# Dealing channels to partitions as 16 x 8 in a DMA-bound batch norm on Trainium2

## The chip, the cores and the metric

The kernel runs on one core of one Trainium2 chip. The metric is the device time of one execution in microseconds (us); lower is better. The kernel before takes 2485.87 us, the median of four runs.

## The reference

A batch norm with given statistics over `x` of shape 32 x 256 x 128 x 128 in float32, 512 MiB in and 512 MiB out:

```python
def reference(x, gamma, beta, running_mean, running_var):
    eps = 1e-5
    ...   # the four parameters reshaped to (1, 256, 1, 1)
    return gamma * (x - mean) / np.sqrt(var + eps) + beta
```

Each channel needs one scale and one shift. All the rest is moving data.

## The kernel before

One tile is half an image: 128 channels, one for each SBUF partition, 16384 elements (64 KiB) a row. There are 64 tiles, three buffers, and one queue (SyncE's) for all loads and stores. Groups of three tiles are loaded, computed in place with one `tensor_scalar` each, and stored.

```python
NBUF = 3
GROUPS = [3] * 20 + [2, 2]
...
    xr = x.rearrange("n (cb p) h w -> (n cb) p (h w)", p=P)
    outr = out.rearrange("n (cb p) h w -> (n cb) p (h w)", p=P)
...
    def load(i):
        t = data.tile([P, HW], f32, tag="t")
        nc.sync.dma_start(out=t[:], in_=xr[i])
        tiles[i] = t
...   # parameters: four rows of 256 loaded, turned in 32x32 blocks, scale and shift computed
    turned = params.tile([B, C], f32, tag="turned")
    nc.vector.transpose(out=turned[:], in_=rows[:])
...
    def store(i):
        t = tiles.pop(i)
        nc.sync.dma_start(out=outr[i], in_=t[:])

    first = 0
    for g, size in enumerate(GROUPS):
        idxs = range(first, first + size)
        for i in idxs:
            compute(i)
        for i in idxs:
            store(i)
        first += size
        ...   # the loads of the next group
```

## Time and profile before

| | before |
|---|---|
| time, median of 4 | 2485.87 us (2485.76 to 2486.37) |
| span of the profiled execution | 2483.6 us |
| VectorE busy | 566.0 us, 23% |
| rate of the DMA engines over the span | 432 GB/s |
| one 64 KiB row on one DMA engine | 2.418 us |

The last line comes from the packet records of the trace, which hold start, duration and size of each packet, but not its engine or addresses. The page and the views behind this, and how the row's time makes up the span, are shown in the prediction. In the same records 16 rows of 64 KiB are in flight for 2417 of the 2484 us, as many as the page counts engines.

### The profile page before, as it was taken

The page shows a single profiled execution, that of the slowest core. Times are in us where ns is not written, and L with a number is a line of the kernel's source. Part 1 is how long each engine was busy: PE and PEld are TensorE (multiplying, and loading weights), DVE is VectorE, ACT ScalarE, POOL GpSimd, SP SyncE. Part 2 cuts the span into 40 slices and gives each one's busy share as a digit, 9 for nine tenths or more (in the row PEclk, how much of TensorE's full clock was granted, in tenths as well). Part 3 has the DMA queues.
Part 4 walks back from the last instruction along what each step waited for, and adds up shares of the span by engine and source line. Part 5 has one row for each costly group of instructions (what it writes and reads, how often), then busy time and mean ns, then how long its engine had stood idle before and what let it go on. Part 6 is the DMA issues. An engine that isn't in the chain of part 4 may idle for free.

```text
span 2483.6 us, 383 instructions
## 1 busy us (share of the span) xinstructions
DVE 566.0 (23%) x75; ACT 1.6 (0%) x2; POOL 0.2 (0%) x4
## 2 busy tenths in 40 slices
DVE  3140404121221213140403121221213040403112
ACT  0000000000000000000000000000000000000000
POOL 0000000000000000000000000000000000000000
DMA  9999999999999999999999999999999999999999
GB/s 421 423 439 439 425 436 439 431 431 439 431 431 439 435 426 436 436 431 435 435 435 427 439 434 427 439 434 427 439 437 432 432 437 433 431 437 433 431 437 396
DMA packets 18442, 1073.77 MB, mean 432 GB/s; under 512 B 2052, under 2 KB 2056, under 8 KB 2056
## 3 DMA queue, kind: packets, MB, share of 16 engines
q1 hardware_dynamic: 18432, 1073.75, 99.9%
q14 instruction: 2, 0.02, 0.0%
q10 hardware_dynamic: 8, 0.00, 0.0%
HBM read 536.88 MB, written 536.87 MB: 432 GB/s over the span
## 4 chain that ended last, share of the span: by engine, by line
another core or an unknown queue 72%; DVE 22%; DMA 4%; issue 0%; DVEq 0%; SPq 0%
DVE t L93 22%; DMA t<-in_x_dram 4%; DVEq L93 0%; SPq L51 0%; SPq L104 0%
## 5 line engine op out<-in xcount | busy, mean ns | idle before, releaser
L93 DVE TENSOR_SCALAR t<-t,scale_t,shift_t 128x16384 f32<-128x16384 f32 x64 | 564.0, 8812 | 1863.9 <-DMA t<-in_x_dram 1863.8
L66 DVE STREAM_TRANSPOSE turned<-rows 32x256 f32<-32x256 f32 x1 | 0.4, 432 | 21.5 <-DMA rows<-in_running_mean_dram 21.5
L78 ACT ACT_TABLE_LOAD x1 | 1.3, 1283 | 2.6 <-issue 2.6
L71 DVE COPY par<-turned 32x8 f32<-32x8 f32 x4 | 0.6, 161 | 0.1
L56 DVE MEMSET rows<- 32x256 f32 x1 | 0.3, 272 | 0.8 <-PEq L132 0.8
L78 ACT ACTIVATE tmp_t<-par,eps_t 128x2 f32<-128x2 f32 x1 | 0.3, 297 | 20.0 <-DVE par L71 20.0
L85 DVE RECIPROCAL tmp_t<-tmp_t 128x2 f32<-128x2 f32 x1 | 0.2, 165 | 0.4 <-ACT tmp_t L78 0.4
L87 DVE TENSOR_TENSOR tmp_t<-par,scale_t 128x2 f32<-128x2 f32 x1 | 0.2, 161 | 0.0
L88 DVE TENSOR_TENSOR shift_t<-par,tmp_t 128x2 f32<-128x2 f32 x1 | 0.2, 161 | 0.0
L86 DVE TENSOR_TENSOR scale_t<-par,tmp_t 128x2 f32<-128x2 f32 x1 | 0.2, 160 | 0.0
L132 POOL MEMSET const-uint8-127<- 128x1 uint8 x1 | 0.1, 103 | 0.0
L132 POOL MEMSET const-bfloat16-1.0<- 128x1 bf16 x1 | 0.1, 101 | 0.0
L132 POOL MEMSET const-float32-0.0<- 128x1 f32 x1 | 0.1, 98 | 0.2 <-issue 0.2
L132 POOL MEMSET const-float32-1.0<- 128x1 f32 x1 | 0.1, 98 | 0.0
L64 DVE MEMSET eps_t<- 128x1 f32 x1 | 0.1, 59 | 0.0
## 6 DMA issues: line engine op xcount, KB each, us to landing
t<-in_x_dram SPq DMA_DIRECT2D x64, 58.0
out_dram<-t SPq DMA_DIRECT2D x64, 49.1
rows<-in_running_var_dram ACTq DMA_DIRECT2D x1, 1.0 KB
rows<-in_gamma_dram ACTq DMA_DIRECT2D x1, 1.0 KB
rows<-in_beta_dram ACTq DMA_DIRECT2D x1, 1.0 KB
rows<-in_running_mean_dram ACTq DMA_DIRECT2D x1, 1.0 KB
```

The costliest lines, as they stand in the source:

```text
L56: nc.vector.memset(rows, 0.0)
L64: nc.vector.memset(eps_t, eps)
L66: nc.vector.transpose(out=turned[:], in_=rows[:])
L71: nc.vector.tensor_copy(out=par[q * B : (q + 1) * B], in_=blocks[:, :, q, 0:4])
L78: nc.scalar.activation(out=tmp_t[:], in_=var_t, func=mybir.ActivationFunctionType.Sqrt, bias=eps_t[:], scale=1.0,)
L85: nc.vector.reciprocal(out=tmp_t[:], in_=tmp_t[:])
L86: nc.vector.tensor_mul(out=scale_t[:], in0=gamma_t, in1=tmp_t[:])
L87: nc.vector.tensor_mul(out=tmp_t[:], in0=mean_t, in1=scale_t[:])
L88: nc.vector.tensor_sub(out=shift_t[:], in0=beta_t, in1=tmp_t[:])
L93: nc.vector.tensor_scalar(out=t[:], in0=t[:], scalar1=scale_t[:, cb : cb + 1], scalar2=shift_t[:, cb : cb + 1], op0=mybir.AluOpType.mult, ...
L132: nc = _bacc.Bacc("TRN2", target_bir_lowering=False, num_devices=1)
```

## The change

The intent is that the 16 DMA engines work side by side on 1 MiB of the tensor. Partition `e * 8 + k` now holds channel `k * 16 + e` of its half, so an engine that takes the eight partitions of one `e` reads channel `e`, then `16 + e`, and so on, while its neighbours read the channels beside it. That each engine takes one `e` is an assumption behind the change; no record names the engine of a packet. The parameters have to be put in the same order, which costs one small VectorE copy.

```diff
-    xr = x.rearrange("n (cb p) h w -> (n cb) p (h w)", p=P)
-    outr = out.rearrange("n (cb p) h w -> (n cb) p (h w)", p=P)
+    NE = 16
+    NK = P // NE
+    xr = x.rearrange("n (cb k e) h w -> (n cb) e k (h w)", k=NK, e=NE)
+    outr = out.rearrange("n (cb k e) h w -> (n cb) e k (h w)", k=NK, e=NE)
...
+    lined = params.tile([B, C], f32, tag="lined")
+    nc.vector.tensor_copy(
+        out=lined.rearrange("p (cb e k) -> p cb e k", e=NE, k=NK),
+        in_=rows.rearrange("p (cb k e) -> p cb e k", k=NK, e=NE),
+    )
     turned = params.tile([B, C], f32, tag="turned")
-    nc.vector.transpose(out=turned[:], in_=rows[:])
+    nc.vector.transpose(out=turned[:], in_=lined[:])
```

## The prediction

> **What bounds the kernel now.** I read the page first (engines, slices, queue), then the group table, then the SyncE queue's own waits, then the windows, and last the single packet records of the trace. The page's top says who is busy:
>
> ```profile
> span 2483.6 us, 383 instructions
> DVE 566.0 (23%) x75; ACT 1.6 (0%) x2; POOL 0.2 (0%) x4
> DMA  9999999999999999999999999999999999999999
> GB/s 421 423 439 439 425 436 439 431 431 439 431 431 439 435 426 436 436 431 435 435 435 427 439 434 427 439 434 427 439 437 432 432 437 433 431 437 433 431 437 396
> q1 hardware_dynamic: 18432, 1073.75, 99.9%
> HBM read 536.88 MB, written 536.87 MB: 432 GB/s over the span
> ```
>
> VectorE works 23% of the span. The DMA engines are at 9 tenths or more in each of the 40 slices, and the one queue that carries the tensor occupies the 16 engines for 99.9% of the span. The rate varies only from 421 to 439 GB/s between the first slice and the last but one. 18432 packets over 128 transfers (64 loads, 64 stores) are 144 each: 128 rows of 64 KiB and 16 small closing packets[...]. So each engine carries 8 rows of a transfer.
>
> ```profile
> L93 DVE TENSOR_SCALAR t<-t,scale_t,shift_t 128x16384 f32<-128x16384 f32 x64 | 564.0, 8812 | 1863.9 <-DMA t<-in_x_dram 1863.8
> t<-in_x_dram SPq DMA_DIRECT2D x64, 58.0
> out_dram<-t SPq DMA_DIRECT2D x64, 49.1
> ```
>
> The compute instruction takes 8.8 us for a tile and waits 1864 us for loads, which costs nothing, since the DMA engines have no gap meanwhile. The waits of the SyncE queue show the same from the other side:
>
> ```profile
> SPq L104 <- DVE t L93: 1451.7, 64, 47.2
> SPq L51 <- DMA out_dram<-t: 950.3, 60, 19.3
> ```
>
> SyncE waits for data, yet three tiles' worth of transfers is always queued ahead of the engines. The windows view, over one group of three tiles in the middle and over the tail, gives the steady rate and the end:
>
> ```profile
> 1000.00:1116.00 116.00, 26.13 (x4) 0.00 (x0) 0.00 (x0) 1.00 1.00 434
> 2453.00:2483.60 30.60, 0.00 (x0) 0.00 (x0) 0.00 (x0) 1.00 0.83 358
> ```
>
> (Columns: length, busy time of VectorE, ScalarE and GpSimd, clock, DMA share, GB/s.) The packet records put a number on one row: of 16384 records of 65536 bytes, 14433 took 2418 ns to the nanosecond and only some 180 took 2450 or more. That is 65536 / 2418 = 27.1 GB/s for an engine, 433.7 for 16. Each engine moves 64 x 2 x 8 = 1024 rows, 1024 x 2.418 = 2476 us. The remaining 7.6 us of the span are start, tail and some slow packets, mostly where a group turns from loads to stores. So the kernel is bound by the pace of one row on one engine, everywhere.
>
> [...]
>
> **The change part by part.**
>
> *Parameters.* One VectorE copy of 32x256 is added. The memset of that shape took 272 ns and the transpose 432 ns, so I estimate 0.3 to 0.45 us with its strided read. It sits before the first tile's compute (25.0 us in the timeline). Then the queue still has two loads to carry, until about 62 us, while the first store is asked for at 33.8 us. Beside work, 0 us on the end.
>
> *Bytes, rows, instructions.* Unchanged: 64 loads and 64 stores, 128 rows of 64 KiB each. The built program writes a load as 128x1x16384 in SBUF from 16x8x16384 in DRAM, where it was 128x16384 on both sides.[...] The issue of a transfer (0.34 us) may grow; with the queue filled ahead it is hidden.
>
> *Addresses in DRAM.* [...] This is the intended gain. But a row already takes 27.1 GB/s, [...] all non-row time is 7.6 us. Gain from it at most 8 us, 0.3%.
>
> *Partitions per engine.* This is where I see the cost. [...] a row takes 2 x 2.418 = 4.836 us. Stores read the same partitions and suffer alike. 1024 x 4.836 = 4952 us, plus 7.6 = 4960 us at worst.
>
> [...] In before, the 16 engines' starts lie within 1 us of each other at first (0.4 of a row) and spread to about 2.4 us (one row) by the end. I take s = 0.4 to 0.7 as a mean: factor 2 - s/4 = 1.9 to 1.83, 2476 x 1.83 to 1.9 = 4530 to 4700, and 4950 with s near 0. The choice is 4750 us.
>
> **The rivals.**
>
> *A: nothing moves.* [...] the engines could fall into opposite phase (s = 4) early and stay there. Then only DRAM addresses differ: 2478 to 2490 us. For it: the intent only makes sense if somebody expected full rate; opposite phase would be kept once reached. Against: nothing in the queue (full at all times) creates such a lead, and the spread in before is a row, not four.
>
> *B: DRAM order hurts.* [...] It would give perhaps 2500 to 2800 us. Unlikely.
>
> *C: partial overlap.* A lead that wanders over all values, mean s = 2, gives factor 1.5: 3720 us. Possible[...].
>
> *D: the intended gain*: 2475 to 2480 us, within 2% in any case; over 2% faster would need 443 GB/s[...].
>
> **Range and chances.** [...] nearly in step (4300 to 4960) 0.62, wandering (3000 to 4300) 0.15, small loss from B 0.04; together slower 0.81. A and D together 0.18; faster by 2%, 0.01. The range 3000 to 4980 leaves out the unmoved kernel, which carries most of the remaining two in ten.
>
> **What would show it right or wrong.** Right: 64 KiB packets at about 4.8 us[...], instead of 2.418; GB/s in the slices 220 to 240; DMA still 9 tenths everywhere; the median landing of loads and stores about doubled (58 to some 110 us, 49 to some 95 us); the wait of L93's instruction for loads at some 4100 us; its 8.8 us unchanged; VectorE's share at 12%. Wandering leads would show as slices that rise in steps from 220 towards 430. B would show packets of mixed length, with reads and writes unequal. The prediction is wrong if packets remain at 2418 ns[...].

The sum: 1024 rows for an engine, each of 2 x 2.418 = 4.836 us, are 4952 us, and with the 7.6 us outside the rows 4960 us at worst. A lead of `s` rows of one engine on another lowers the factor of 2 by `s / 4`, so `s` of 0.4 to 0.7 gives 2476 x 1.83 to 1.9 = 4530 to 4700 us; opposite phase is a lead of four rows, half of the eight that an engine carries of a transfer. The choice was 4750 us. The factor of 2 and `s / 4` are assumptions, and only the row of 2.418 us, the 16384 rows over 16 engines and the 7.6 us come from the trace. The gain of at most 8 us likewise assumes that a row does not get shorter than 2.418 us. The 2500 to 2800 us of rival B are a guess.

## The result

The changed kernel takes 4587.2 us, the median of four runs (4549.3 to 4651.2). The ratio is 1.840, with a 95% interval of 1.828 to 1.852. A ratio is the mean time of one kernel's fast runs over that of the other's of the same rounds, so it is not quite the ratio of the medians quoted here. The profiled execution is the slowest of the four (4651 us). It is labelled slow because it lies more than 1.5% above the fastest; this kernel scatters by that much by itself, and the readings below are about a factor of nearly two.

The page of the changed kernel, the lines that answer to the first ones of before:

```profile
span 4649.2 us, 384 instructions
DVE 566.4 (12%) x76; ACT 1.6 (0%) x2; POOL 0.2 (0%) x4
DMA  9999999999999999999999999999999999999998
GB/s 208 235 211 257 235 252 226 228 240 223 239 219 246 226 240 219 241 224 240 227 232 230 226 239 224 245 227 251 223 241 223 240 235 233 233 229 244 201 223 204
q1 hardware_dynamic: 18432, 1073.75, 98.8%
HBM read 536.88 MB, written 536.87 MB: 231 GB/s over the span
```

The engines are as busy as before and the packets and bytes are the same, yet the rate is 231 GB/s in place of 432. So no wait was added; each packet takes longer. "Busy" in this view only says that a packet was in flight: the queue is at 98.8% at this rate.

The groups and the issues (after the bar: busy us, mean ns, then idle time before it; for an issue, the median us to landing):

```profile
L102 DVE TENSOR_SCALAR t<-t,scale_t,shift_t 128x16384 f32<-128x16384 f32 x64 | 564.0, 8812 | 3984.6 <-DMA t<-in_x_dram 3984.6
L70 DVE COPY lined<-rows 32x256 f32<-32x256 f32 x1 | 0.4, 364 | 38.3 <-DMA rows<-in_running_mean_dram 38.3
t<-in_x_dram SPq DMA_DIRECT2D x64, 113.5
out_dram<-t SPq DMA_DIRECT2D x64, 93.9
```

The compute instruction is unchanged at 8812 ns and waits 3985 us for loads, where it waited 1864. Landing went from 58.0 to 113.5 us for a load and from 49.1 to 93.9 for a store. Both directions suffer. The SyncE queue's own waits grew in the same proportion:

```profile
SPq L113 <- DVE t L102: 2724.0, 64, 83.6
SPq L55 <- DMA out_dram<-t: 1785.1, 60, 38.0
```

The parameters are not the cause. The timeline at the first tile:

```profile
39.41 0.36 DVE L70 COPY lined<-rows 32x256 f32<-32x256 f32 x1 [38.29 <-DMA rows<-in_running_mean_dram]
...
41.92 0.16 DVE L97 TENSOR_TENSOR shift_t<-par,tmp_t 128x2 f32<-128x2 f32 x1
44.30 8.81 DVE L102 TENSOR_SCALAR t<-t,scale_t,shift_t 128x16384 f32<-128x16384 f32 x1 [2.22 <-DMA t<-in_x_dram]
```

The added copy took 0.36 us and the shift was ready at 42 us. The first tile's data came only at 44.3 us, so the compute waited for data, not for parameters.

The packet records show the new term. In the first three loads (384 rows) the median row took 5.11 us and the shortest 4.21. Over the whole run the median is 4.99 us: 11834 of 16384 rows took 4.5 us or more, 1880 under 2.5 us, the rest between. Each transfer leaves 16 small closing packets, and as many semaphore events, in the trace; the first compute starts 0.1 us after the last of the 16 events of its load (44.2 and 44.3 us). Since there are 16 for each transfer and 16 rows in flight, I take them as one for each engine; the records name none. From the last of one transfer to the last of the next, the mean time is 39.1 us for a load and 33.5 for a store, where before it was 19.4 and 19.3. (The expectations below use 38.1 and 34.2. Those come from the closing packets in order of time, sixteen at a time, which mixes neighbouring transfers.) By this reading the engines do not stay together either. The closing packets of one load lie within 1.0 us in the first three loads and about 40 us apart by the seventh. Over all 128 transfers the median is 59 us, more than the 41 us that eight rows of 5.11 us take. Before, it was never over 4.2 us.

### The profile page after: what moved, and what is told of

The parts are those of the page before. It is cut to its first block, busy times and chain, and to the rows that moved or that the text cites. A ratio compares the mean times of both kernels' runs of the same rounds, so it can differ in the third digit from the quotient of the medians.

```text
span 4649.2 us, 384 instructions
## 1 busy us (share of the span) xinstructions
DVE 566.4 (12%) x76; ACT 1.6 (0%) x2; POOL 0.2 (0%) x4
## 3 DMA queue, kind: packets, MB, share of 16 engines
q1 hardware_dynamic: 18432, 1073.75, 98.8%
## 4 chain that ended last, share of the span: by engine, by line
another core or an unknown queue 86%; DVE 12%; DMA 1%; issue 0%; DVEq 0%
DVE t L102 12%; DMA t<-in_x_dram 1%; DVEq L102 0%
## 5 line engine op out<-in xcount | busy, mean ns | idle before, releaser
L102 DVE TENSOR_SCALAR t<-t,scale_t,shift_t 128x16384 f32<-128x16384 f32 x64 | 564.0, 8812 | 3984.6 <-DMA t<-in_x_dram 3984.6
## 6 DMA issues: line engine op xcount, KB each, us to landing
t<-in_x_dram SPq DMA_DIRECT2D x64, 113.5
out_dram<-t SPq DMA_DIRECT2D x64, 93.9
```

Of the source, the lines that this page charges most:

```text
L102: nc.vector.tensor_scalar(out=t[:], in0=t[:], scalar1=scale_t[:, cb : cb + 1], scalar2=shift_t[:, cb : cb + 1], op0=mybir.AluOpType.mult, ...
```

## The experiments

My theory was that the partitions are the cause: that some sets of partitions, when the engines reach them at the same time, slow the rows down. The main rival was the DRAM order: that rows which stand 64 KiB apart, side by side, are slower. A third suspect is the issue, which the change lengthened: the median record of a load on the SyncE queue went from 339 to 577 ns. No trace names the partition or the engine of a packet, so the theories can only be told apart by kernels.

The mechanism that I had in mind for the theory, and the name that went with it, are cut from the expectations below, since no run shows them. A forecast that follows a cut without a name is that of this theory. A pair is two engines that, by the theory, slow each other down; a lead is the head start of one on the other, in rows.

**The same deal, another DRAM order.**

```diff
-    xr = x.rearrange("n (cb k e) h w -> (n cb) e k (h w)", k=NK, e=NE)
+    xr = x.rearrange("n (e cb k) h w -> n cb e k (h w)", cb=NCB, e=NE)
```

(The output and the parameters follow.) The 16 steps of the pattern now stand 1 MiB apart in DRAM, each of eight neighbouring channels.

> The deal of the change (16 x 8 rows[...]) with another DRAM order[...]. [...] as slow as the change, 4450 to 4750 us, packets again in two heaps at 2.42 and about 5.05 us. DRAM-order theory (side-by-side 64 KiB steps hurt): near 2486 us, at most 2600.

It took 4544.9 us (2 runs), ratio 1.827; the results are correct. The slices of its page:

```profile
GB/s 211 230 212 265 229 269 232 236 246 228 243 221 252 227 253 227 243 228 239 235 235 240 230 243 225 257 220 253 225 259 231 234 234 238 241 228 246 209 226 207
```

The side-by-side order is gone and the loss stays. The packets are as in the changed kernel (11513 rows of 4.5 us or more, 2088 under 2.5), not in two clean heaps.

**Nearly the changed DRAM order, the plain 128 partitions.**

```diff
-    xr = x.rearrange("n (cb p) h w -> (n cb) p (h w)", p=P)
+    xr = x.rearrange("n (hf b c) (q h2) w -> (n hf) (c q) b (h2 w)", hf=2, b=4, q=4)
```

A partition holds a quarter channel of four channels; the scale table has eight columns and the compute is cut in four.

> The DRAM order of the change, nearly, with the plain 128-partition deal: a partition holds a quarter (16 KiB) of a channel[...], rows of 16 KiB. [...] 2475 to 2500 us, rows of 16 KiB at about 0.605 us. DRAM-order theory: slow, 3500 us or more.

It took 2506.5 us (4 runs), ratio 1.0078 (1.0062 to 1.0095), correct. That is just above my 2475 to 2500.

```profile
GB/s 410 431 430 431 430 431 429 431 431 431 430 430 431 430 432 429 431 430 431 430 431 430 431 430 431 431 430 431 430 431 430 431 430 432 430 431 429 431 430 379
```

Blocks of four partitions that stand 64 KiB apart in DRAM run at nearly the full rate, 429 GB/s over the span against 432. The 0.8% fits the shorter rows: four of 16 KiB take 4 x 0.611 = 2.444 us against 2.418 for one of 64 KiB. The order is only nearly that of the change, but the two runs together rule the side-by-side order out as the cause of the loss, and the halves below find the same loss in the DRAM order of before. A gain from it is not visible either.

**Engines set apart in time.** If the loss comes from what the engines reach at the same time, a head start for some of them should change it. I chose four rows, half of the eight that an engine carries of a transfer. Two small copies from DRAM to DRAM, queued first, are meant to delay 12 engines by four rows and then 4 of these by four more (the trace has 12 and then 4 closing packets for them, which I read as so many engines; it does not say which):

```diff
+    LEAD = 4
+    scratch = nc.dram_tensor("scratch", (16, LEAD + 1, HW), f32).ap()
+    images = x.rearrange("n c h w -> n c (h w)")
+    nc.sync.dma_start(out=scratch[4:16, 0:LEAD], in_=images[4:16, 0:LEAD])
+    nc.sync.dma_start(out=scratch[0:4, 0:LEAD], in_=images[0:4, 0:LEAD])
```

> The changed kernel with two small DRAM-to-DRAM copies queued ahead of everything, one on 12 engines and one on 4 of them[...]. [...] opposite phase, so 2500 to 2900 us, most packets at 2.42 us. DRAM-order theory[...]: 4400 to 4750 us as before.

It took 2631.0 us (2 runs), ratio 1.058, correct. The transfers, addresses and partitions are those of the changed kernel, and 1956 us of the loss are gone. The slices:

```profile
GB/s 346 423 419 437 430 430 430 430 431 430 432 429 433 429 430 426 426 434 426 434 426 434 429 428 433 427 433 430 431 429 436 432 429 433 430 430 314 238 225 201
```

The full rate holds for 36 slices and then falls to the changed kernel's. The closing packets of a transfer say why. Up to the last load before the stores of the first group of two tiles, the first of the last four closing packets comes 18.4 to 19.6 us after the first of all. Then these groups dissolve within one transfer. In the timeline there:

```profile
2398.07 8.81 DVE L108 TENSOR_SCALAR t<-t,scale_t,shift_t 128x16384 f32<-128x16384 f32 x1 [68.87 <-DMA t<-in_x_dram]
2406.91 19.94 SPq L119 DMA_DIRECT2D out_dram<-t  x2
```

The first store of the group is issued at 2406.9 us, when eleven of the 16 closing packets of the second and last load of the group are already out. I read this so: these eleven engines have nothing left to do and start this store together, and so the head start is lost. The transfers are slow from there on (314, 238, 225 and 201 GB/s in the last slices). They do not stay in step: the next two loads close over 45 us.

**The same with groups of three to the end.** `GROUPS = [3] * 21 + [1]`.

> The lead of 4 rows again, with groups of three tiles to the end and one tile last, in place of two groups of two. In the run with lead 4 the completions of a transfer kept the same spread until the first group of two, 2404 us, and lost it there: the leading engines run dry, because one queued tile (19.4 us) does not cover the spread (19.6 us) plus a compute (8.8 us), and then all start together. If that is the reason: 2500 to 2550 us. If the lead dies out of itself by that time: 2600 us or more.

It took 2561.7 us (4 runs, 2551 to 2582), ratio 1.031 (1.026 to 1.037), correct. That is just above my band of 2500 to 2550.

```profile
GB/s 335 413 420 432 432 434 432 436 431 433 432 436 432 433 433 427 433 429 433 432 430 432 432 431 429 434 428 432 428 435 431 426 435 429 430 432 436 426 416 146
```

The spread now stays until the last tile, whose lone store has nothing queued beside it and falls into the slice of 146 GB/s. So the reason given for the loss at the groups of two fits, and opposite phase does not die out by itself in 2.4 ms (426 to 436 GB/s from the fourth slice to the 38th). It does not beat the kernel before.

**A head start of two rows, and of eight.** The same diff with `LEAD = 2` and `LEAD = 8`.

> The same with a lead of 2 rows. [...] eight rows at a lead of s rows take 2 x (s x 2.42 + (4 - s) x 5.05) us, so 128 transfers at s = 2 take about 3825 us; with some drift 3300 to 4200 us. Theory without kept leads: 4400 to 4750 us.

> A lead of 8 rows, one whole turn of a transfer[...]. [...] 4400 to 4750 us, as without a lead. If any long lead frees the engines (for example by the distance in DRAM): 2500 to 2900 us.

Two rows: 4515.9 us (2 runs), correct. My rule, an estimate from fast rows of 2.42 us and slow ones of 5.05, by which the gain grows evenly with the head start, is wrong. It is not that the lead vanished at once: the closing packets of the second and third loads still come in groups 5 to 6 us apart. Yet between 50 and 100 us no row took less than 4.31 us, against 2.418 in before. This head start does not free these loads at all. (Its 5 to 6 us are two rows at the fast pace but only about one at 5 us a row; no other lead under four rows was tried.) The run is also the control for the copies themselves: with copies queued ahead, the time is still within 2% of the changed kernel's.

Eight rows: two runs, 2718.0 and 4332.0 us, correct. The midpoint means nothing; one execution went each way.

> The same kernel as the run with lead 8, whose two executions took 2718 and 4332 us, for its spread. If a pair can fall into opposite phase by chance and then stays: again a mix of executions near 2700 and near 4300 to 4600 us. If a long lead frees the engines as such: all near 2700. If one of the two executions was a disturbance: all like the other.

The four runs took 4427.7, 4416.5, 2720.0 and 4305.1 us. The granted clock is 1.0 in all, and both kinds came again: this kernel has two ways to go. Of six executions four stay near the changed kernel (two of them, 4305 and 4332 us, just below my band of 4400 to 4750) and two are near 2720 us. One of each kind was profiled, first the one of 2718 us, then the one of 4427.7:

```profile
GB/s 257 279 392 357 413 414 423 427 419 432 417 432 417 430 423 418 430 418 434 421 422 429 418 433 417 438 418 426 429 418 433 418 431 419 429 423 396 287 234 167
GB/s 239 364 315 335 286 252 258 253 223 243 220 254 218 254 221 254 223 252 223 247 224 246 225 243 232 242 232 234 236 233 237 232 239 229 246 225 248 209 226 211
```

In the first, the second transfer closes in three groups, at 0, 35 to 38 and 48 to 51 us; by the tenth, which closes at 278 to 293 us, the 16 lie within 15 us, and from then on the rate is 413 GB/s or more until near the end. The second starts with the same groups, reaches 364 GB/s, and loses it again. So a long lead as such does not free the engines. That some fall into opposite phase by chance fits both traces, but it is a reading and not shown: once the fast state lasted, and once the beginning of it did not.

**Both halves of the engines in step.** In the run with two rows, one slow row could have kept the others slow too (the common hold-up of the expectation). A third copy, of six rows on 8 engines, is meant to put one half of the engines a whole transfer of eight rows behind the other, with a lead of two rows inside each half, so that both halves do the same at the same moment:

```diff
+    nc.sync.dma_start(out=scratch[16:24, 0 : 8 - LEAD], in_=images[16:24, 0 : 8 - LEAD])
```

> The run with lead 2 was slow throughout (4516 us), and rows stayed at 4.3 to 5.15 us [...]. Here a third copy on 8 engines (6 rows) [...]. Common hold-up: rows of 2.42 us appear in the first three loads (a quarter to a half of them), and the run may fall into opposite phase: 2500 to 4000 us. If a lead under 4 rows never frees anything: 4400 to 4750 us, no row under 2.7 us in the first 100 us.

It took 4531.1 us (2 runs), correct. Some fast rows stand in the first 50 us, while some engines are still at the copies, but between 50 and 100 us the median is 4.97 us and none is below 3.2. The closing packets put the halves 21 us apart and the engines of a half 5 us. 21 us are about eight rows at the copies' pace but four at 5 us a row, so the halves are in step only if the pattern repeats every four rows, which no run shows. With that reserve, a common hold-up is not supported, and why two rows help nothing stays open.

**Loads alone, stores alone.** Only `xr` as changed, or only `outr`; the output is in a permuted channel order. Their outputs are wrong, which doesn't matter for the times.

> The loads as changed, the stores as before; the output is in a permuted channel order, so wrong on purpose. The changed kernel took 38.1 us for a load and 34.2 for a store on average. [...] 64 x (39 to 40 + 19.4) = 3740 to 3800 us. DRAM-order theory has been ruled out for both together; if only stores had the cost: 2486 us.

> The stores as changed, the loads as before; output wrong on purpose. With 34.2 us for a store as in the changed kernel: 64 x (34.2 + 19.4) = 3430 us; 3350 to 3700. Sum rule with the loads-only run: the two excesses over 2486 should add up to about 2080 us, the whole loss, if loads and stores suffer independently.

Loads alone: 3832.1 us (2 runs), ratio 1.541, somewhat above my 3740 to 3800. Stores alone: 3360.3 us (2 runs), ratio 1.351. The excesses over 2486.8 of the same rounds are 1345 and 874 us, 2219 together against a whole loss of 2101 (my sum rule had about 2080), so they nearly add up. Landing in the run with loads alone:

```profile
t<-in_x_dram SPq DMA_DIRECT2D x64, 100.6
out_dram<-t SPq DMA_DIRECT2D x64, 69.8
```

Landing times include the queue ahead, so both grow (the unchanged stores from 49.1 to 69.8 us). The closing packets separate them: a load takes 40.6 us and a store 19.3 in this run, 19.7 and 32.7 in the other. Reading SBUF and writing SBUF are both hit, loads harder. In the run with loads alone 7687 rows took 4.5 us or more, of 8192 that are loads, although the engines lie 43 to 55 us apart from the 22nd load to the 62nd. This spread stays the same within a group of three loads or three stores and doubles where stores turn to loads (5.9 to 10.7, 11.0 to 21.3, 21.3 to 42.6 us).

**64 partitions at a time, two ways.** This takes the kernel before and leaves the 16 x 8 shape out. Each transfer is cut in two, by adjacent halves or by even and odd partitions:

```diff
-        nc.sync.dma_start(out=t[:], in_=xr[i])
+        for h in range(2):
+            nc.sync.dma_start(out=t[64 * h : 64 * h + 64], in_=xr[i, 64 * h : 64 * h + 64])
```

and, in the other kernel, `t[h::2]` and `xr[i, h::2]`; stores alike.

> The kernel before with each transfer cut in two: partitions 0 to 63 and 64 to 127, DRAM order unchanged. [...] 4300 to 4960 us. If the loss comes from the 16 x 8 shape or its DRAM order alone: 2486 to 2510 us.

> The same cut in two, but into even and odd partitions[...], with the same number of transfers and rows as the run with partitions 0 to 63. [...] 2485 to 2500 us. If [...] the smaller transfer is what costs: 4300 us or more.

Adjacent halves took 4608.6 us (2 runs), ratio 1.853. Even and odd took 2489.6 us (4 runs), ratio 1.001 (0.9995 to 1.0025). Both are correct. First adjacent, then even and odd, from the queue line of the page, its slices, and the tile view (duration of an issue in ns, minimum, median, maximum):

```profile
q1 hardware_dynamic: 20480, 1073.76, 99.0%
GB/s 210 224 227 273 260 243 239 225 239 220 247 219 264 220 248 220 240 238 233 239 230 239 226 251 226 255 219 242 224 248 231 238 235 226 235 226 246 202 223 207
L52 SPq DMA_DIRECT2D t<-in_x_dram x128: 465/590/2686, 0.7 to 4410.6; - x128
```

```profile
q1 hardware_dynamic: 20480, 1073.76, 99.8%
GB/s 419 423 438 438 435 425 437 436 436 427 435 437 435 426 437 437 433 428 436 437 434 427 437 437 434 427 437 435 433 430 434 438 432 430 436 438 430 429 438 368
L52 SPq DMA_DIRECT2D t<-in_x_dram x128: 471/589/1359, 0.7 to 2390.4; - x128
```

The same packets, bytes, number of transfers and issue time; only the set of partitions in a transfer differs, and with it the DRAM rows. One runs at half the rate. The issue time is cleared as well: 589 ns costs nothing at 2489.6 us. And the changed kernel's time is found again without its shape, which points to the partitions that are reached at one time.

## Why the prediction was right

The choice was 4750 us; the result, 4587.2, is 3.4% below it.

**What bounds the kernel.** Right. The packets did not change in number or bytes, and the row's duration set the time: 64 x (39.1 + 33.5) = 4646 us of the span of 4649. One reading was too strong: three tiles' worth is not always queued ahead. In before, two transfers were outstanding for 611 us of the span and one for 56.

**Parameters.** Right: 0.36 us against 0.3 to 0.45, and beside work.

**Issue.** Right that it may grow (339 to 577 ns) and that it is hidden; the even and odd halves show it with twice as many transfers.

**Addresses in DRAM.** Right that they matter little, though the floor of 2.418 us a row, on which the gain of at most 8 us rests, was assumed. The run with the plain 128 partitions takes 2506.5 us with nearly the changed order, and the run with another order has the whole loss, which disposes of rival B.

**Partitions per engine.** This was the step that carried the forecast, and it was right in its outcome; its reason was not shown. That two sets of 64 partitions differ by 1.85 to 1.00, and that a head start of four rows takes the changed kernel from 4587 to 2631 us (2562 with groups of three to the end), is shown. Together they point to the partitions that are reached at the same time. Which partitions an engine gets, and what in the chip slows them, no record shows.

**The size of the conflict.** The forecast assumed 2 x 2.418 = 4.836 us for a row in conflict. Measured was 5.11 us in the first loads, 6% more. That by itself would have given 1024 x 5.11 = 5233 us.

**The lead.** Here a step failed, and it hid the first error. The prediction assumed that a lead is kept, since nothing changes it, and that the gain grows evenly with it, to a factor of 1.83 to 1.9. The loads deny the even growth: with two rows of lead they gained nothing, and in the changed kernel a load cost 39.1 / 19.4 = 2.02 times as much. That nothing changes a lead holds within loads: the 16 closing packets lie within 1.1 us in all of the first three, and 14.6, 14.6 and 13.8 us apart in the next three. It is false of stores, where they spread to 2.3, 5.4 and 10.0 us in the first three and the mean factor was 33.5 / 19.3 = 1.73.

The lead that was put in was misread too. The starts in before, sorted sixteen at a time, cannot show more than about a row, which would explain the 2.4 us; the closing packets of each transfer lie 0.6 us apart at first and 4.2 (1.7 rows) at the end. And the state that the forecast thought most likely, nearly in step, held for three loads only: then the engines moved apart by a median of 59 us. The measured total lies inside the 4530 to 4700 of that step because two errors cancel: the row in conflict was taken too short (4.84 us against 5.11), and what the engines gain by not being in step too small (5 to 8.5% in the forecast; 12% measured, 4587 us of 5233). That number was luck and was not earned by its mechanism.

**Rival A** was wrong for this kernel but right in one clause: opposite phase, once reached, was kept for 2.4 ms in the two kernels with a lead of four rows. **Rival C**, leads that wander and a factor of 1.5: the engines did wander, over more than a whole turn, but the factor stayed at 1.84. Whether any two engines stay close meanwhile cannot be seen, since no record names an engine.

Most of the listed signs came out: landings of 113.5 and 93.9 us against some 110 and 95, a wait of 3985 us against 4100, VectorE at 12%. The slices are wider than said, 201 to 257 GB/s against 220 to 240, and not all packets are near 4.8 us: the median is 4.99, and 11% of the rows (1880) were still under 2.5.

What stays open: what in the chip slows the rows, why a row in conflict takes over twice its time alone (5.11 us against 2.418), why loads gain nothing from a lead of two rows or from engines that are far apart, while four rows free them, and what spreads the engines.

## What to carry to other kernels

When a DMA-bound kernel is at the pace of a single row on each engine, as here (1024 x 2.418 us of 2483.6), ask of any new access pattern first which partitions a transfer reaches at the same time (1.853 against 1.001 for two sets of 64), and only then how it lies in DRAM (1.827 for the change in another order). A load and a store with the 128 partitions as the slowest dimension on both sides, as in the kernel before, took 2486 us here; the 16 x 8 split took 4587 and nearly halved the rate (231 GB/s against 432) while the engines still looked busy (98.8%), so read GB/s and packet durations, not the busy share. If a tile must be moved in two transfers of 64 partitions, try even and odd ones, which took the same time here as one transfer of 128 (ratio 1.001), where adjacent halves took 1.853 times as long.
